# A softmax kernel: tiles of 15, 7 and 3 rows per partition instead of 16, 8 and 4

## The chip, the cores and the metric

The kernel runs on one core of a Trainium2 chip. Its time is the device time of one execution in microseconds. Before the change it is 163.14 us, the median of four runs (163.02 to 163.36). The program is written for the core's engines directly: VectorE (DVE in the profile), ScalarE (ACT), GpSimd (POOL) and SyncE (SP) each run their own list of instructions, TensorE (PE) has no work, and 16 DMA engines move data between HBM and the on-chip memory SBUF, which has 128 partitions.

## The reference

A softmax over the last axis, with a temperature of 2, on 16 x 1024 rows of 512 float32 values:

```python
x_scaled = x / 2.0                      # x: (16, 1024, 512) float32
x_max = np.max(x_scaled, axis=-1, keepdims=True)
exp_x = np.exp(x_scaled - x_max)
return exp_x / np.sum(exp_x, axis=-1, keepdims=True)
```

So 33.55 MB are read once and 33.55 MB written once, and there are 16384 independent rows, 128 for each partition.

## The kernel before, in words

One SBUF tensor, `arena`, holds 100 rows of 512 values per partition (200 KB). Everything happens in place in it: a row is loaded, replaced by its exponentials, scaled, and stored from the same address.

The list `PLAN` (lines 11 to 14) says how the 128 rows of each partition are cut. Each entry is one tile: the rows of its compute chunks, and the row of the arena where it begins. A tile of `r` rows is one load and one store. It takes `r * 128` consecutive rows of the input, and partition `p` gets the `r` consecutive rows `p*r` to `p*r + r - 1` of them (`dram`, a rearrangement "(p r) d -> p r d"). For one partition that is one unbroken piece of HBM, `r` times 2 KB long, and the pieces of neighbouring partitions lie that far apart.

Before the change there are 11 tiles: 4, 8, five times 16, 8, 16, 8 and 4 rows, all computed in chunks of 4 rows. The first eight fill the arena's 100 rows exactly. The last three (16, 8 and 4 rows) use the places of tiles 2, 1 and 0 again: the dictionary `behind` holds, for each tile, the earlier tiles whose place it overlaps.

For each chunk of rows:

- VectorE takes the maximum of each row, negated (`do_max`, line 85: one reduce for the chunk). It waits until the tile's load has landed.
- ScalarE computes exp(0.5 * x + negmax) row by row and gathers each row's sum (line 111). The first row of a chunk waits for the chunk's maximum.
- VectorE takes the reciprocals of the sums (line 94) and multiplies each row by its own (line 98, `do_mul`).

VectorE's order is written out: the maximum of chunk k, then the reciprocals and multiplies of chunk k - 2 (`LAG = 2`).

The transfers are on two queues. The loads of the first eight tiles are issued by ScalarE (line 81), one after the other, before its first exponential. The first two of them are put into the program's entry block ahead of the barrier at which the engines meet. All stores (line 134) are issued by SyncE in tile order, each after a wait for the tile's last multiply. The late loads (line 139) are issued by SyncE too. After the store of tile t, SyncE issues every late load whose overlapped tiles are t - 2 or older, each after a wait for the store of the overlapped tile to have landed. In the kernel before, all three late loads follow the store of tile 4. At the end SyncE waits for all stores.

Everything that a transfer's size, a tile's place and the order of the late loads need is worked out from `PLAN`; no other line knows how long a tile is.

Of the kernel before, what the change touches and what calls it, by code (L numbers as in the profile page):

```python
# [1 line left out]

# [4 lines left out]

PLAN = [
    ([4], 0), ([4, 4], 4), ([4] * 4, 12), ([4] * 4, 28), ([4] * 4, 44), ([4] * 4, 60),
    ([4] * 4, 76), ([4, 4], 92), ([4] * 4, 12), ([4, 4], 4), ([4], 0),
]
ARENA = 100
LAG = 2


@with_exitstack
def kernel(  # L20
    ctx: ExitStack,
    tc: tile.TileContext,
    x: bass.AP,
    out: bass.AP,
):
    nc = tc.nc
    fp32 = mybir.dt.float32

    xf = x.flatten_outer_dims()
    of = out.flatten_outer_dims()  # L30
    N, D = xf.shape
    P = nc.NUM_PARTITIONS
    n_rows = N // P
    assert sum(sum(c) for c, _ in PLAN) == n_rows

    arena = nc.alloc_sbuf_tensor("arena", (P, ARENA, D), fp32)
    negmax = nc.alloc_sbuf_tensor("negmax", (P, n_rows), fp32)
    sums = nc.alloc_sbuf_tensor("sums", (P, n_rows), fp32)
    recip = nc.alloc_sbuf_tensor("recip", (P, n_rows), fp32)

    tiles, chunks, base = [], [], 0
    for t, (cs, at) in enumerate(PLAN):
        r = sum(cs)
        tiles.append((base, r, at))
        o = 0
        for c in cs:
            chunks.append((t, base + o, c, at + o))
            o += c  # L50
        base += r
    last_chunk = {c[0]: k for k, c in enumerate(chunks)}

    def dram(ap, t):
        b, r, _ = tiles[t]
        return ap[b * P : (b + r) * P].rearrange("(p r) d -> p r d", r=r)

    def sb(t):
        _, r, at = tiles[t]
        return arena[:, at : at + r, :]  # L60


    behind = {}
    for t, (_, r, at) in enumerate(tiles):
        for u in range(t):
            _, ru, au = tiles[u]
            if at < au + ru and au < at + r:
                behind.setdefault(t, []).append(u)

    ld = [tc.alloc_semaphore(f"ld{t}") for t in range(len(tiles))]  # L70
    st = [tc.alloc_semaphore(f"st{t}") for t in range(len(tiles))]
    s_max = tc.alloc_semaphore("s_max")
    s_exp = tc.alloc_semaphore("s_exp")
    s_rec = tc.alloc_semaphore("s_rec")
    s_mul = tc.alloc_semaphore("s_mul")

    def issue_loads(begin, end):

        for t in range(begin, end):
            if t not in behind:  # L80
                nc.scalar.dma_start(out=sb(t), in_=dram(xf, t)).then_inc(ld[t], 16)

    def do_max(k):
        t, b, c, a = chunks[k]
        nc.vector.reduce_max(  # L85
            out=negmax[:, b : b + c],
            in_=arena[:, a : a + c],
            axis=mybir.AxisListType.X,
            negate=True,
        )._wait_ge(ld[t], 16).then_inc(s_max, 1)  # L90

    def do_mul(k):
        t, b, c, a = chunks[k]
        nc.vector.reciprocal(  # L94
            out=recip[:, b : b + c], in_=sums[:, b : b + c]
        )._wait_ge(s_exp, k + 1).then_inc(s_rec, 1)
        for r in range(c):
            ins = nc.vector.tensor_scalar_mul(  # L98
                out=arena[:, a + r],
                in0=arena[:, a + r],  # L100
                scalar1=recip[:, b + r : b + r + 1],
            )
            if r == 0:
                ins._wait_ge(s_rec, k + 1)
        ins.then_inc(s_mul, 1)

    def compute_and_store():

        for k, (t, b, c, a) in enumerate(chunks):
            for r in range(c):  # L110
                ins = nc.scalar.activation(  # L111
                    out=arena[:, a + r],
                    in_=arena[:, a + r],
                    func=mybir.ActivationFunctionType.Exp,
                    bias=negmax[:, b + r : b + r + 1],
                    scale=0.5,
                    accum_out=sums[:, b + r : b + r + 1],
                )
                if r == 0:
                    ins._wait_ge(s_max, k + 1)  # L120
            ins.then_inc(s_exp, 1)


        for k in range(len(chunks) + LAG):
            if k < len(chunks):
                do_max(k)
            if k >= LAG:
                do_mul(k - LAG)


        late = sorted(behind)
        for t in range(len(tiles)):
            nc.sync.wait_ge(s_mul, last_chunk[t] + 1)
            nc.sync.dma_start(out=dram(of, t), in_=sb(t)).then_inc(st[t], 16)  # L134
            while late and max(behind[late[0]]) <= t - 2:
                u = late.pop(0)
                for v in behind[u]:
                    nc.sync.wait_ge(st[v], 16)
                nc.sync.dma_start(out=sb(u), in_=dram(xf, u)).then_inc(ld[u], 16)
        for t in range(len(tiles)):  # L140
            nc.sync.wait_ge(st[t], 16)

    hook = nc.inst_callbacks[-1]
    nc.remove_inst_callback(hook)
    symbolic = nc._always_lower_symbolic_ap
    nc._always_lower_symbolic_ap = False
    here = str(nc.cur_bb)
    entry = nc.main_func.blocks[0]  # L150
    head, jumps = entry.instructions[:-5], entry.instructions[-5:]
    entry.instructions = []
    nc.switch_bb("main", None)
    issue_loads(0, 2)
    first = list(entry.instructions)
    at = next(k for k, i in enumerate(head) if type(i).__name__ == "InstDrain")
    entry.instructions = head[:at] + first + head[at:]
    issue_loads(2, len(tiles))
    compute_and_store()
    entry.instructions = list(entry.instructions) + jumps  # L160
    nc.switch_bb(here, None)
    nc._always_lower_symbolic_ap = symbolic
    nc.push_inst_callback(hook)


# [1 line left out]
_INS = ['x']  # L167
_OUTS = [((16, 1024, 512), 'float32')]


# [23 lines left out]
```

## Time and profile before

| | |
|---|---|
| median of 4 runs | 163.14 us (163.02 to 163.36) |
| the profiled execution | 163.47 us, of which the span is 161.7 us |
| VectorE busy | 127.0 us (79%), 192 instructions |
| ScalarE busy | 95.0 us (59%), 257 instructions |
| DMA | 67.14 MB, mean 415 GB/s over the span |
| reduce of a chunk of 4 rows (line 85) | 32 of 2279 ns |
| multiply of a row (line 98) | 128 of 481 ns |
| exponential of a row (line 111) | 128 of 710 ns, and 187 ns to read its sum |

The profile shows one execution. "Busy" counts the time in which an engine runs an instruction. In lines that describe a group of instructions, the part after the last bar is the engine's idle time just before them and what ended it. A queue's share is the time of its packets as a part of 16 DMA engines' span; a packet is what one DMA engine moves in one go. In the lines of transfers the last number is the time from issue to landing, which includes the time in which the transfer stands behind others in its queue. In a table of stretches the columns are: begin and end, length, busy time (and count) of VectorE, ScalarE and GpSimd, TensorE's granted clock, the DMA engines' share, and GB/s.

### The profile page before, as it was taken

To read this page: it belongs to the slowest core of one execution; us is meant where nothing else is said; L and a number is where in the kernel's file an instruction comes from. 1 tells how busy PE (TensorE), PEld (TensorE's weight loads), DVE (VectorE), ACT (ScalarE), POOL (GpSimd) and SP (SyncE) were. 2 spreads that over 40 slices of the span, in tenths; PEclk is the share of its full clock that TensorE was granted. 3 is DMA by queue.
4 is the path that set the end of the run, shared out by engine and by line. 5 is a ranking of instruction groups with operands and counts; after the bars stand their busy time and mean duration, and the time that the engine had idled before them with its cause. 6 is when DMAs were issued, how large, how long until landed. Compare 5 with 4: busy or idle time off the path is not lost.

```text
span 161.7 us, 518 instructions
## 1 busy us (share of the span) xinstructions
DVE 127.0 (79%) x192; ACT 95.0 (59%) x257; POOL 0.2 (0%) x4
## 2 busy tenths in 40 slices
DVE  0559199999999999999966999998999999920000
ACT  0559457777777777777771777775777777600000
POOL 0000000000000000000000000000000000000000
DMA  6999999999989999999999999999999999999993
GB/s 243 462 462 389 401 466 454 367 397 462 462 375 503 389 422 446 438 413 422 462 405 409 458 422 440 413 442 389 373 434 454 430 422 420 446 434 446 397 407 136
DMA packets 3172, 67.14 MB, mean 415 GB/s; under 512 B 352, under 2 KB 352, under 8 KB 352
## 3 DMA queue, kind: packets, MB, share of 16 engines
q1 hardware_dynamic: 2016, 40.90, 59.3%
q10 hardware_dynamic: 1152, 26.21, 38.3%
q14 instruction: 4, 0.03, 0.0%
HBM read 33.55 MB, written 33.55 MB: 415 GB/s over the span
## 4 chain that ended last, share of the span: by engine, by line
DVE 54%; DMA 33%; issue 0%; DVEq 0%; SPq 0%
DMA arena<-in_x_dram 33%; DVE negmax L85 29%; DVE arena L98 24%; DVE recip L94 1%; DVEq L189 0%; SPq L134 0%
## 5 line engine op out<-in xcount | busy, mean ns | idle before, releaser
L111 ACT ACTIVATE arena<-arena,negmax 128x512 f32<-128x512 f32 x128 | 90.8, 710 | 40.8 <-DVE negmax L85 40.8
L85 DVE TENSOR_REDUCE negmax<-arena 128x4 f32<-128x2048 f32 x32 | 72.9, 2279 | 14.4 <-DMA arena<-in_x_dram 14.4
L98 DVE TENSOR_SCALAR arena<-arena,recip 128x512 f32<-128x512 f32 x128 | 53.6, 481 | 1.1
L111 ACT ACTIVATION_READ_ACCUMULATOR arena<-arena,negmax 128x1 f32 x128 | 23.9, 187 | 0.0
L94 DVE RECIPROCAL recip<-sums 128x4 f32<-128x4 f32 x32 | 5.4, 168 | 0.0
L111 ACT ACT_TABLE_LOAD x1 | 1.3, 1283 | 4.3 <-issue 4.3
L178 POOL MEMSET const-bfloat16-1.0<- 128x1 bf16 x1 | 0.1, 103 | 0.0
L178 POOL MEMSET const-uint8-127<- 128x1 uint8 x1 | 0.1, 102 | 0.0
L178 POOL MEMSET const-float32-0.0<- 128x1 f32 x1 | 0.1, 98 | 0.2 <-issue 0.2
L178 POOL MEMSET const-float32-1.0<- 128x1 f32 x1 | 0.1, 98 | 0.0
## 6 DMA issues: line engine op xcount, KB each, us to landing
out_dram<-arena SPq DMA_DIRECT2D x6, 4096.0 KB, 26.3
arena<-in_x_dram ACTq DMA_DIRECT2D x5, 4096.0 KB, 45.1
out_dram<-arena SPq DMA_DIRECT2D x3, 2048.0 KB, 20.4
arena<-in_x_dram ACTq DMA_DIRECT2D x2, 2048.0 KB, 53.3
arena<-in_x_dram SPq DMA_DIRECT2D x1, 4096.0 KB, 35.0
out_dram<-arena SPq DMA_DIRECT2D x2, 1024.0 KB, 17.6
arena<-in_x_dram SPq DMA_DIRECT2D x1, 2048.0 KB, 38.5
arena<-in_x_dram ACTq DMA_DIRECT2D x1, 1024.0 KB, 4.8
```

Of the source, the lines that this page charges most:

```text
L85: nc.vector.reduce_max(out=negmax[:, b : b + c], in_=arena[:, a : a + c], axis=mybir.AxisListType.X, negate=True,)._wait_ge(ld[t], 16).the ...
L94: nc.vector.reciprocal(out=recip[:, b : b + c], in_=sums[:, b : b + c])._wait_ge(s_exp, k + 1).then_inc(s_rec, 1)
L98: ins = nc.vector.tensor_scalar_mul(out=arena[:, a + r], in0=arena[:, a + r], scalar1=recip[:, b + r : b + r + 1],)
L111: ins = nc.scalar.activation(out=arena[:, a + r], in_=arena[:, a + r], func=mybir.ActivationFunctionType.Exp, bias=negmax[:, b + r : b + r ...
L178: nc = _bacc.Bacc("TRN2", target_bir_lowering=False, num_devices=1)
```

## The change

Only `PLAN` changes. The tiles become 3, 7, six times 15, 15, 7, 3 and 3 rows: twelve instead of eleven. The chunks have 5 rows in the 15-row tiles, 4 and 3 in the 7-row tiles, and 3 in the 3-row tiles: 28 chunks instead of 32. The first eight tiles again fill the arena's 100 rows and are loaded by ScalarE. The four late tiles (15, 7, 3 and 3 rows) use the places of tiles 2, 1 and 0 and the first three rows of tile 3's place. By the rule for late loads, the first three follow the store of tile 4, and the twelfth tile's load follows the store of tile 5.

```diff
 PLAN = [
-    ([4], 0), ([4, 4], 4), ([4] * 4, 12), ([4] * 4, 28), ([4] * 4, 44), ([4] * 4, 60),
-    ([4] * 4, 76), ([4, 4], 92), ([4] * 4, 12), ([4, 4], 4), ([4], 0),
+    ([3], 0), ([4, 3], 3), ([5] * 3, 10), ([5] * 3, 25), ([5] * 3, 40), ([5] * 3, 55),
+    ([5] * 3, 70), ([5] * 3, 85), ([5] * 3, 10), ([4, 3], 3), ([3], 0), ([3], 25),
 ]
```

## The prediction

> **What bounds the kernel now.** I read four views in this order: the slices, to see which resource never rests; the queues and transfers, to see what it carries; the stretches, to find where it loses time; then the chain of waits and the store issues, to see whether compute ever starves it.
>
> The slices (40 of 4.04 us each; digits are tenths of busy time):
>
> ```profile
> DVE  0559199999999999999966999998999999920000
> ACT  0559457777777777777771777775777777600000
> DMA  6999999999989999999999999999999999999993
> DMA packets 3172, 67.14 MB, mean 415 GB/s; under 512 B 352, under 2 KB 352, under 8 KB 352
> ```
>
> The DMA row is full from the second slice to the last but one, while VectorE falls silent four slices before the end. The 16 DMA engines are the bound; VectorE's end is not the kernel's. The chain that ended last gives "DVE 54%", but it ends in the last multiply at 142.5 us, with 19 us of span to come, so I don't take it for the bound.
>
> The queues and transfers (q10 is ScalarE's queue: the first eight loads; q1 is SyncE's: all stores and the late loads):
>
> ```profile
> q1 hardware_dynamic: 2016, 40.90, 59.3%
> q10 hardware_dynamic: 1152, 26.21, 38.3%
> ...
> out_dram<-arena SPq DMA_DIRECT2D x6, 4096.0 KB, 26.3
> arena<-in_x_dram ACTq DMA_DIRECT2D x5, 4096.0 KB, 45.1
> ```
>
> 59.3% + 38.3% = 97.6% of 161.7 us: 157.8 us of packets on each engine. The trace's packet records show one packet per partition and transfer (8, 16 or 32 KB, eight per engine), with medians of 309, 611 and 1213 ns, and 9 ns for each semaphore packet. The three lie on a line: (1213 - 309)/3 = 301.3 ns for 8 KB, and 309 - 301.3 = 7.7 ns fixed.
>
> The ideal sum for one engine is then 32 x 309 + 48 x 611 + 96 x 1213 + 22 x 9 = 155.86 us. The rest of the span: the first packet starts at 1.15; packets above their median add 2.12 us per engine; engines without a packet, about 0.3. That makes 159.4, where the last store's sixteen landings have their mean (159.43); the slowest engine lands at 160.60; 1.08 us of closing waits follow: 161.7. So the change can act through the packet sum, the 2.4 us of slow packets and gaps, or the 1.17 us by which the slowest engine trails the mean, unless it starves the DMA.
>
> The stretches (us; the last two columns are DMA share and GB/s):
>
> ```profile
> 63.00:96.00 33.00, 30.09 (x45) 22.21 (x62) 0.00 (x0) 1.00 1.01 433
> ...
> 113.00:115.00 2.00, 1.97 (x7) 1.74 (x5) 0.00 (x0) 1.00 0.93 397
> 115.00:117.00 2.00, 2.00 (x2) 1.19 (x4) 0.00 (x0) 1.00 1.04 344
> 117.00:119.00 2.00, 1.97 (x7) 1.75 (x5) 0.00 (x0) 1.00 1.10 463
> 119.00:135.00 16.00, 15.86 (x26) 11.77 (x33) 0.00 (x0) 1.00 1.00 432
> ```
>
> Steady traffic makes 432 or 433 GB/s. The largest dip is at 115 to 117, 344 GB/s at a full share. That is the last late load (tile 10, 4 rows), alone on q1 between another load and the store of tile 5: 30 of its 128 packets take 319 to 1048 ns instead of 309. Mean landings of the two loads lie 3.19 us apart (114.96 and 118.15) where 8 packets need 2.48: 0.7 us lost. The spread of the sixteen landings grows there from 1.48 to 2.32 us, and every store after it keeps 2.3.
>
> Last, waits and two store issues:
>
> ```profile
> DVE negmax L85 <- DMA arena<-in_x_dram: 14.4, 5, 5.0
> ...
> 110.18 0.34 SPq L134 DMA_DIRECT2D out_dram<-arena  x1
> ...
> 134.99 0.33 SPq L134 DMA_DIRECT2D out_dram<-arena  x1
> ```
>
> Tile 6's store is issued at 110.18, while its predecessor in the ring lands at 129.1; tile 8's at 134.99, its predecessor at 143.6. The least slack late in the run is thus 8.6 us.
>
> **The change, part by part.**
>
> *Packets.* The bytes stay. Now 3-, 7- and 15-row tiles give packets of 6, 14 and 30 KB: by the line above 234, 535 and 1138 ns, an estimate from those three medians. Per engine: 6 transfers of 3 rows (48 x 233.7 = 11.22), 4 of 7 (32 x 535.0 = 17.12), 14 of 15 (112 x 1137.7 = 127.42), 24 semaphore packets (0.22): 155.97 us, +0.11. All of it is on the path.
>
> A rule speaks louder against more and smaller transfers: the Trainium skill, "DMA: Bandwidth & Descriptors", section "Rules for kernel authors", wants at least 1 MiB per DMA, and its "Anatomy of one DMA" gives each a fixed 2 us or so. The 3-row transfers are 0.75 MiB, and two transfers are added: by that rule an estimated +4 us, 167. The row says otherwise: transfers queue behind one another and the DMA share stays at 1.00 across their borders, so the fixed time is covered, and I take 0.11. It would show only if a ring ran dry.
>
> *A twelfth tile.* Its 3 rows go to row 25 of the arena, so its load waits for the store of tile 3. SyncE issues that load after store 5 and ahead of store 6; on q1 it lies between two stores. The nearest row is the dip above: a small load on q1 alone, with a store behind it, lost 0.7 us on the mean engine. Bounds: nothing, if that dip was tied to its moment; 1.1 us, what the slowest engine lost there (last landings 3.57 us apart against 2.48). I take the row, scaled to 3 rows of 4: +0.5. Gains are not excluded for the traffic as a whole, but for these 3 rows I see no reason for one.
>
> The wait itself: behind it on SyncE stand store 6 and later ones. Store 5 needs 70 rows computed. By the chain, 4 rows take 2.19 + 0.10 + 0.03 + 1.68 = 4.0 us of VectorE, so 70 rows are ready near 90. Store 3 covers 40 rows, where the present one covers 44 and landed at 86.3. The semaphore is up; price nothing, and store 6 has over 10 us in hand were it late.
>
> *Starvation.* VectorE does one row per 1.0 us, the DMA one per 1.21 (load plus store). With 5-row chunks, a reduce lies between 2279 ns (the 4-row price) and 2849 (in proportion); four chunks fewer save small fixed costs, hidden under DMA. The waits move: tile 7 has 15 rows, not 8. Loads arrive at one row per 1.2 us while stores share evenly, so tile 6 lands near 80 and tile 7 near 98; VectorE comes to them near 76 and 95 and waits about 4 us each, against 2.7 and nothing now. Store 6 is then issued near 109, store 7 near 124, store 8 near 137, the last near 146. On q1, when q10 ends near 98, the ring holds 25 late rows, store 5 (15) and the twelfth load (3): 43 x 0.607 us = 26, to 124. Store 6 then lasts to 133, store 7 to 142. So store 8 has about 5 us in hand rather than 8.6. Price nothing; with 6 us more of waiting, each further us would be a us of time.
>
> *Start and end.* The first load is 3 rows: VectorE starts some 0.6 us earlier, which nothing waits for, because q10 keeps the engines full. The first packet still starts at 1.15. One more final wait costs about 0.03.
>
> *Addresses.* Partitions now lie 30 KB apart in HBM, not 32. The row: slow packets come in clusters where a transfer starts or ends (18.9, 29.4 to 33.5, 97 to 100 us), 1.1 us per engine outside the first burst and the dip at 115. If they come from streams stepping together at power-of-two distances, they could go, with part of the 1.17 us of spread: a gain of 0 to 2.3. [...] The trace has 433 GB/s at 32 KB, and most packets at their median. [...] The other way, a packet that isn't a multiple of 8 KB might be slower; no row has one; 1% on the 30 KB packets would cost 1.3 us. Between these I take 0, where the rows of full rate stand.
>
> Sum: +0.11 + 0.5 + 0.03 = +0.64 on the profiled span, 161.7 to 162.3. The profiled execution took 163.47, so 1.8 us lie around the span; it was 0.33 above the median of the runs. Added to that median: 163.14 + 0.64 = 163.8 us.
>
> **The rivals.**
>
> *The odd pitch pays.* For it: the clusters, in which all 16 engines are slow at once, and the lag of the slowest engine. Against it: tile 2's load also starts in step on all engines, without slow packets. Half of clusters and lag gives -1.15, with the +0.64 above: 162.6; all of it, with a harmless twelfth load: 161.0. It decides once 0.97 us is won (0.64 + 0.33).
>
> *The twelfth load is free* and the dip was a matter of its moment: +0.14, 163.3; within 0.2% (0.33 us, about what a measurement of this kernel can tell from no change).
>
> *The DMA starves or the odd packets are slow.* VectorE's longer waits push store 8 past 142, or 30 KB packets lose 1%: 165 or more. Against it: 5 us of slack and the straight line of packet times.
>
> **How the numbers follow.** Slower by the sum (163.5 to 164.4): 0.44; free twelfth load: 0.18; pitch pays: 0.31; starvation or slow packets: 0.07. The likeliest gives 163.8, with its own range 163.5 to 164.4. The range for 8 in 10 takes in most of the pitch case: 162.0 to 164.6. Faster 0.31; same 0.18; slower 0.51.
>
> **What would show it.** Right: packets, less the slow ones, at 234, 535 and 1138 ns; a DMA row full to the end; a second dip in GB/s near 122 to 126, where the twelfth load runs; last landings spread by over 2.3 us. Wrong: no slow packets near transfer borders and a spread under 1.5 us (the pitch), or a slice of the DMA row below 9 between 100 and 150 us (starvation). The forecast fails if packet times leave their line, since each 1% of them weighs 1.6 us.

## The result and the profile after

The changed kernel takes 162.78 us (median of 44 runs, 162.14 to 164.08) against 163.40 of the kernel before in the same sessions (63 runs): a ratio of 0.9966, 95% interval 0.9954 to 0.9977. It is 0.34% faster, where 163.8 us, 0.64 us more than before, was forecast. The median lies inside the range of 162.0 to 164.6, but on the other side of "no change". Its profiled execution has a span of 160.8 us, against 161.7. A few executions take 2 us or more longer, whatever the kernel (166.53 and 166.84 us among the 63), and the ratios leave these out.

The slices of the changed kernel, with its packet count:

```profile
DVE  0475599999999999999799919999999999950000
ACT  0739087866697666886287634668766875600000
DMA  7999999999999999999999999999999999999993
DMA packets 3459, 67.13 MB, mean 418 GB/s; under 512 B 384, under 2 KB 384, under 8 KB 1152
```

The DMA row is full again, now without the one slice of 8 that the kernel before has. VectorE shows a deep hole in its 24th slice and still ends before the DMA. So the bound is the same, and nothing starved it.

The queues and transfers of the changed kernel:

```profile
q1 hardware_dynamic: 2304, 40.90, 59.3%
q10 hardware_dynamic: 1152, 26.21, 38.7%
...
out_dram<-arena SPq DMA_DIRECT2D x7, 3840.0 KB, 26.1
arena<-in_x_dram ACTq DMA_DIRECT2D x6, 3840.0 KB, 48.1
```

By the packet records of these two queues, an engine has 157.53 us of packets, where it had 157.93. The sum by the measured medians (234, 535 and 1138 ns) rises by 0.16 us, so it is the slow packets that became fewer or shorter: 1.50 us per engine lie above the medians instead of 2.06.

The stretches of the changed kernel (DMA share and GB/s at the end). Its late load of tile 10 lands at 113.47 us, so the place to compare is 111 to 113, not 115 to 117:

```profile
63.00:96.00 33.00, 27.97 (x43) 21.82 (x60) 0.00 (x0) 1.00 1.01 433
...
109.00:111.00 2.00, 2.00 (x6) 2.00 (x7) 0.00 (x0) 1.00 0.92 388
111.00:113.00 2.00, 2.00 (x1) 1.07 (x4) 0.00 (x0) 1.00 1.20 492
113.00:115.00 2.00, 1.97 (x6) 1.63 (x5) 0.00 (x0) 1.00 1.00 430
...
119.00:121.00 2.00, 2.00 (x5) 2.00 (x7) 0.00 (x0) 1.00 0.78 335
121.00:123.00 2.00, 2.00 (x1) 0.93 (x4) 0.00 (x0) 1.00 1.19 501
123.00:125.00 2.00, 1.96 (x7) 1.77 (x5) 0.00 (x0) 1.00 0.98 418
125.00:127.00 2.00, 2.00 (x2) 1.86 (x6) 0.00 (x0) 1.00 1.00 430
```

A packet is counted where it starts, so neighbours must be read together: 388 and 492 make 440 GB/s. In the kernel before, 397, 344 and 463 from 113 to 119 make 401. The landings say it more sharply: tiles 9 and 10 land on the mean 1.95 us apart, where their packets need 1.88; before it was 3.19 against 2.48. The dip is gone. Nor is there one where the twelfth load runs: 335 and 501 make 418 GB/s, and 418 and 430 follow.

VectorE's waits for loads and two store issues of the changed kernel:

```profile
DVE negmax L85 <- DMA arena<-in_x_dram: 15.7, 5, 4.6
...
105.70 0.34 SPq L134 DMA_DIRECT2D out_dram<-arena  x1
...
133.68 0.33 SPq L134 DMA_DIRECT2D out_dram<-arena  x1
```

Store 8 is issued at 133.68; its predecessor in the ring (the queue's list of packets) lands at 142.70. That is 9 us in hand, no less than before.

The account that the rest of this document uses splits each profile's end into four parts. A transfer lands on each of the 16 engines at its own time; the mean is over the sixteen. "Lag at tile 9" is the mean landing of that late load, less the first packet's start and less its own packets and all those queued ahead of it, by their medians. "Dip" is what the next load, tile 10, adds to that lag. "Rest" is what is added until the last store's mean landing. "Last" is how far the slowest DMA engine trails that mean.

| profile | lag at tile 9 | dip | rest | last | span |
|---|---|---|---|---|---|
| before | 1.84 | 0.71 | -0.13 | 1.17 | 161.7 |
| before, again (e1) | 2.22 | 0.65 | -0.13 | 1.12 | 162.0 |
| after | 1.64 | 0.07 | -0.26 | 1.08 | 160.8 |
| after, again (e2) | 1.60 | 0.08 | -0.28 | 0.89 | 160.6 |
| after, third (e16) | 1.64 | 0.09 | -0.25 | 1.66 | 161.4 |

By their means: lag -0.41, dip -0.60, rest -0.13, last +0.07, first packet and packets +0.16. The sum is -0.91 us; the mean spans differ by -0.90. So the gain has two main parts: 0.60 us is one event of some 2 us length, 0.41 is spread over the 110 us before it. These few profiles show more than the times do, whose medians differ by 0.62 us. Two profiles of the kernel before differ by 0.38 in their lag alone, so the part of the dip is the surer one.

### The profile page after: what moved, and what is told of

It reads as the page before. It is cut to its first block, busy times and chain, and to the rows that moved or that the text cites. A ratio compares the mean times of both kernels' runs of the same rounds, so it can differ in the third digit from the quotient of the medians.

```text
span 160.8 us, 513 instructions
## 1 busy us (share of the span) xinstructions
DVE 126.3 (79%) x184; ACT 94.5 (59%) x257; POOL 0.2 (0%) x4
## 4 chain that ended last, share of the span: by engine, by line
DVE 74%; DMA 10%; another core or an unknown queue 3%; issue 0%; DVEq 0%
DVE negmax L85 40%; DVE arena L98 32%; DMA arena<-in_x_dram 10%; DVE recip L94 2%; DVEq L189 0%
## 5 line engine op out<-in xcount | busy, mean ns | idle before, releaser
L85 DVE TENSOR_REDUCE negmax<-arena 128x5 f32<-128x2560 f32 (+2 forms) x28 | 72.3, 2585 | 15.7 <-DMA arena<-in_x_dram 15.7
L94 DVE RECIPROCAL recip<-sums 128x5 f32<-128x5 f32 (+2 forms) x28 | 4.9, 176 | 0.0
```

The source lines that it names most:

```text
L85: nc.vector.reduce_max(out=negmax[:, b : b + c], in_=arena[:, a : a + c], axis=mybir.AxisListType.X, negate=True,)._wait_ge(ld[t], 16).the ...
L94: nc.vector.reciprocal(out=recip[:, b : b + c], in_=sums[:, b : b + c])._wait_ge(s_exp, k + 1).then_inc(s_rec, 1)
```

## The experiments

All kernels here are read in the same account. Times are ratios to the kernel before, run on the same chip in the same session.

### Does the dip come every time?

e1 is the kernel before and e2 the changed kernel, both unchanged. e1 and, further down, e9 are single executions; the others were timed 4 to 13 times.

> The kernel before, unchanged, for a second profile. Three theories of the 0.9 us of span that the change won. LATE LOAD: the gain is the vanished dip at the late 4-row load (tile 10), where the kernel before fell 0.7 us behind its packet sum. PITCH: the 15-row tiles cure slow packets along the whole run. MOMENT: the dip was an accident of one execution. LATE LOAD expects the dip here again: mean landings of tiles 9 and 10 about 3.2 us apart (2.48 by the packets), some 30 slow 8 KB packets, spread of the last landings 2.3 us. PITCH expects slow packets again before 100 us (1.1 us per engine), the dip either way. MOMENT expects 2.5 us between the two landings and a last spread near 1.5.

Measured: span 162.0 us, dip 0.65 us, last landings spread over 2.36 us. The stretches of this second profile:

```profile
113.00:115.00 2.00, 1.97 (x6) 1.33 (x4) 0.00 (x0) 1.00 0.94 401
115.00:117.00 2.00, 2.00 (x3) 1.60 (x6) 0.00 (x0) 1.00 0.98 340
117.00:119.00 2.00, 1.97 (x6) 1.35 (x4) 0.00 (x0) 1.00 1.09 434
```

340 GB/s at the same place, where the first profile had 344: the theory of a mere moment falls.

> The changed kernel, unchanged, for a second profile and a time on the same chip as the two kernels beside it. All theories: ratio to before 0.9966 or so (0.995 to 0.998). LATE LOAD and PITCH: no dip at tiles 10 and 11 again (mean landings of tiles 9 and 10 within 0.1 us of the 1.88 that the packets need). MOMENT: a dip may appear at any place.

Measured: 162.83 us, ratio 0.9963 (0.9942 to 0.9983), dip 0.08 us, span 160.6.

### Is it the late load's size?

e3 gives the kernel before a late load of 3 rows; e4 gives the changed kernel one of 4 rows.

```diff
 # e3, on the kernel before
-    ([4] * 4, 76), ([4, 4], 92), ([4] * 4, 12), ([4, 4], 4), ([4], 0),
+    ([4] * 4, 76), ([4, 4], 92), ([4] * 4, 12), ([5, 4], 3), ([3], 0),
 # e4, on the changed kernel
-    ([5] * 3, 70), ([5] * 3, 85), ([5] * 3, 10), ([4, 3], 3), ([3], 0), ([3], 25),
+    ([5] * 3, 70), ([5] * 3, 85), ([5] * 3, 10), ([3, 3], 4), ([4], 0), ([3], 25),
```

> The kernel before with one thing changed: the late tiles have 16, 9 and 3 rows instead of 16, 8 and 4, so the last late load is the 3-row load of the changed kernel; everything before it keeps 16, 8 and 4. LATE LOAD: most of the gain comes back, ratio 0.996 (0.994 to 0.998), the landings of tiles 9 and 10 are 1.9 us apart, last spread under 1.9. PITCH: no gain, ratio 1.000 (0.998 to 1.002), slow packets before 100 us as before. MOMENT: ratio 1.000.

> The changed kernel with one thing changed: the late tiles have 15, 6, 4 and 3 rows instead of 15, 7, 3 and 3, so the last load ahead of store 5 is a 4-row one with 8 KB packets, as in the kernel before; the twelfth tile stays. LATE LOAD: the gain is lost, ratio near 1.000 (0.998 to 1.002), the landings of tiles 9 and 10 are 3.1 us apart instead of 2.48. PITCH: the gain stays, ratio 0.9966, landings 2.5 us apart. MOMENT: as the changed kernel, 0.9966.

Measured: e3 has a ratio of 0.9997 (0.9970 to 1.0024), a dip of 0.67 us and a lag of 2.15; e4 has 0.9958 (0.9938 to 0.9979), a dip of 0.06 and a lag of 1.62. Both go against the theory of the late load. The size of that load, 3 or 4 rows, does nothing to the mean; the gain stays with the 15-row tiles. The same stretches of e3, with 6 KB packets in the dip:

```profile
113.00:115.00 2.00, 1.97 (x6) 1.52 (x5) 0.00 (x0) 1.00 0.95 409
115.00:117.00 2.00, 2.00 (x2) 1.41 (x4) 0.00 (x0) 1.00 1.02 322
117.00:119.00 2.00, 1.97 (x6) 1.53 (x5) 0.00 (x0) 1.00 1.18 465
```

### Is it the packets or the addresses?

e5 and e6 keep all sizes and the order, and change only which rows of HBM a tile takes: each partition owns 128 consecutive rows, so the pieces of all tiles lie 256 KB apart. e7 does the like on e3, with 250 KB for all tiles but the last, tile 10, whose pieces keep to 6 KB.

```diff
 # e5 on the kernel before, e6 on the changed kernel
-        return ap[b * P : (b + r) * P].rearrange("(p r) d -> p r d", r=r)
+        return ap.rearrange("(p n) d -> p n d", p=P)[:, b : b + r, :]
 # e7 on e3
+        if b + r <= 125:
+            return ap[: 125 * P].rearrange("(p n) d -> p n d", p=P)[:, b : b + r, :]
         return ap[b * P : (b + r) * P].rearrange("(p r) d -> p r d", r=r)
```

> The kernel before with another cut of the HBM side alone: every partition owns 128 consecutive rows, so all tiles have a pitch of 256 KB between partitions; packets, tile sizes, order and waits stay. Three theories of what the 15-row tiles cure, now that the size of the late load is out. PITCH: streams that step together at a power-of-two distance collide; 256 KB is a higher power of two, so it is as slow as before or slower: ratio 1.000 to 1.02, dip at 115 to 117 us as before or deeper. PACKET: it is the 32 KB packets (or the 30 KB ones) whatever the address; ratio 1.000 (0.998 to 1.002). STORE BEHIND: the dip comes from the 16-row store that follows the late load; ratio 1.000, dip as before.

> The changed kernel with the same other cut: a pitch of 256 KB for all tiles, 15-row tiles and 30 KB packets as they are. PITCH: the gain is lost, ratio equal to that of the kernel before with 256 KB (1.000 to 1.02), a dip and clusters of slow packets like those of the kernel before. PACKET and STORE BEHIND: the gain stays, ratio 0.996 (0.994 to 0.998), no dip.

> The kernel before with late tiles of 16, 9 and 3 rows (0.9997 of before), and the HBM side cut so that each partition owns 125 consecutive rows for all tiles but the last: a pitch of 250 KB, no power of two, with 32 KB packets and all else kept. PITCH: the gain appears without any 15-row tile: ratio 0.996 (0.994 to 0.998), no dip at 115 to 117 us. PACKET and STORE BEHIND: ratio 1.000 (0.997 to 1.002), the dip stays.

| | ratio | lag at tile 9 | dip |
|---|---|---|---|
| e5: 16 rows, 256 KB | 0.9969 (0.9945 to 0.9992) | 1.66 | 0.37 |
| e6: 15 rows, 256 KB | 0.9992 (0.9971 to 1.0013) | 1.66 | 0.29 |
| e7: 16 rows, 250 KB | 0.9993 (0.9971 to 1.0015) | 1.78 | 0.52 |

The changed kernel gets a dip back as soon as its addresses change, with the very same packets; on the slowest engine it is 1.26 us (last landings of tiles 9 and 10 at 111.56 and 114.70, less 1.88). The stretches of e6 show it at 111 to 113:

```profile
109.00:111.00 2.00, 2.00 (x4) 2.00 (x7) 0.00 (x0) 1.00 0.95 385
111.00:113.00 2.00, 1.99 (x2) 0.71 (x3) 0.00 (x0) 1.00 1.08 393
113.00:115.00 2.00, 1.97 (x5) 2.00 (x6) 0.00 (x0) 1.00 1.05 455
```

So the dip depends on where the rows lie in HBM, and packet size alone does not decide. At 256 KB the two kernels have the same lag and nearly the same dip, and the 15-row tiles are even slower (163.38 us in e6 against 162.97 in e5, same session): 15 rows win nothing there by themselves. But it isn't "powers of two" either: stores 250 KB apart keep the dip, and the kernel before became faster at 256 KB, where that theory said slower or equal. No theory had expected that. The lag at tile 9 is 1.84 to 2.22 us in the profiles with 16-row pieces 32 KB apart, and 1.66 and 1.78 with the other two pitches, on one profile each: by these, the smaller part of the gain comes with getting away from pieces 32 KB apart, not with 15 rows.

How far apart the engines are before the load does not decide either: the sixteen landings of tile 9 spread over 1.48 us in the kernel before, 1.43 in e6, and 1.90 in e11 below, which has no dip.

### What makes the dip?

e8 gives tile 5, whose store stands right behind the last late load, 15 rows in the kernel before (and tile 7 nine). e9 makes SyncE hold that store back until the load has landed.

```diff
 # e8
-    ([4] * 4, 60), ([4] * 4, 76), ([4, 4], 92),
+    ([5] * 3, 60), ([4] * 4, 75), ([5, 4], 91),
 # e9
             nc.sync.wait_ge(s_mul, last_chunk[t] + 1)
+            if t == 5:
+                nc.sync.wait_ge(ld[10], 16)
```

> The kernel before with two sizes changed: tile 5 has 15 rows instead of 16, tile 7 has 9 instead of 8; the store of tile 5, which stands behind the last late load, then has 30 KB pieces at a 30 KB pitch. STORE BEHIND: the dip at 115 to 117 us goes (mean landings of tiles 9 and 10 2.5 us apart), ratio 0.997 (0.995 to 0.999). PACKET: only one tile in six differs, ratio 0.9995, dip stays. PITCH: the dip goes if the store is its half of the collision, and stays if the load alone makes it.

> The kernel before, where SyncE holds the store of tile 5 back until the last late load (tile 10) has landed, so that no write to HBM is under way while that load is read. SWITCH (the dip is made by engines that already write tile 5 while others still read tile 10): the slow 8 KB packets at 115 to 117 us go, tiles 9 and 10 land 2.5 us apart on the mean, and the span grows only by the DMA's rest between the two, some 2 us, to 163 to 165. LOAD ALONE (small packets slow by themselves): some 30 slow packets stay.

e9 is the clearest run of the study. Its dip is -0.02 us, and the packets of 8 KB on q1 exceed their median by 0.04 us per engine instead of 0.50. The wait and the stretches of e9:

```profile
SPq L135 <- DMA arena<-in_x_dram: 38.9, 1, 38.9
...
115.00:117.00 2.00, 2.00 (x3) 1.90 (x6) 0.00 (x0) 1.00 0.90 381
117.00:119.00 2.00, 1.97 (x5) 1.04 (x3) 0.00 (x0) 1.00 0.24 98
```

SyncE stands 38.9 us in front of store 5 and issues it at 119.05, where the kernel before does so at 94.23. The engines run dry from 117 on (share 0.24), which costs more than the dip: span 163.8. But the load's packets keep their pace to the end. So, by this one execution, the load alone is not slow; it is slow when the store stands behind it in the ring. How the store does it is not shown. The theory named engines that already write while others still read. But in the kernel before, the lengthened packets start between 115.25 and 117.8 us, and the first packet of store 5 at 116.72: a third of the loss (0.16 of 0.49 us per engine) lies in packets that had ended by then, and only 0.05 in packets that started later.

e8's time was 0.9980 (0.9948 to 1.0012); repeated as e15 it was 0.9974 (0.9957 to 0.9991). The executions profiled were longer than that (span 164 and 166 us), and show a dip of about 0.5 us; what a shorter one has is not known.

> The kernel before with 15 rows in tile 5 and 9 in tile 7 once more, since its first profile was of a disturbed execution. TILE PITCH: dip under 0.1 us between tiles 9 and 10, ratio 0.997. BASE PARITY: dip of 0.4 to 0.6 us (all regions up to tile 5 still begin on multiples of 1 MB), ratio 0.998 to 1.000.

By the time, one tile of 15 rows in place of 16 wins about 0.2%, between the theories; by these two profiles it doesn't cure the dip. It settles nothing.

### Loads or stores?

e10 and e11 give the 256 KB pitch to one side only, in the changed kernel. Their output has its rows in another order; the work is the same.

```diff
+        if ap is xf:    # e10; e11: "if ap is of"
+            return ap.rearrange("(p n) d -> p n d", p=P)[:, b : b + r, :]
         return ap[b * P : (b + r) * P].rearrange("(p r) d -> p r d", r=r)
```

> The changed kernel with loads cut at a pitch of 256 KB between partitions and stores as they are (30, 14 and 6 KB): the rows of the output come out in another order, the work is the same. LOAD SIDE (the addresses that are read make the dip): a dip at tile 10 as with 256 KB on both sides (0.3 us on the mean, last landing 1.2 us late), ratio 0.999. STORE SIDE: no dip (under 0.1 us), ratio 0.9965. BOTH (only the pair of patterns counts): neither is full.

> The changed kernel with stores cut at a pitch of 256 KB and loads as they are; the rows of the output come out in another order, the work is the same. LOAD SIDE: no dip, ratio 0.9965. STORE SIDE: the dip of 256 KB on both sides, ratio 0.999.

Measured: e10 0.9965 (0.9936 to 0.9994), dip 0.01 us; e11 1.0006 (0.9976 to 1.0036), dip 0.05. Neither side alone brings the dip back. Both sides together do (e6). So, on one profile each, it is a matter of reads and writes against each other. One pair of runs doesn't fit a rule of the pitches alone: e7 and e11 both load tile 10 in 6 KB pieces and store 250 or 256 KB apart, yet e7 with 16 rows has a dip of 0.52 us and e11 with 15 rows 0.05. That e11 has no dip and yet no gain I can't explain by the dip: its slowest engine trails the mean by 1.55 us, against 0.9 to 1.7 in the changed kernel, and its interval still reaches into that of the changed kernel.

### The place of the regions

e12 takes the rows of tile 10 from the front of HBM in the kernel before. e13 shifts the beginnings of the regions of tiles 2 to 7 and 10 to odd multiples of 256 KB (tile 8, which the expectation counts in, stays on a multiple of 1 MB), by a 7-row tile 1, a 9-row tile 7 and late tiles of 16, 7, 4 and 1. e14 orders the changed kernel's regions so that those of tiles 5 and 10 begin at multiples of 1 MB.

```diff
 # e12
+        b = 0 if t == len(tiles) - 1 else b + tiles[-1][1]
 # e13
+    ([4], 0), ([4, 3], 4), ([4] * 4, 11), ([4] * 4, 27), ([4] * 4, 43), ([4] * 4, 59),
+    ([4] * 4, 75), ([5, 4], 91), ([4] * 4, 11), ([4, 3], 4), ([4], 0), ([1], 27),
 # e14
+        order = [2, 3, 4, 6, 5, 7, 8, 1, 10, 0, 9, 11]
+        b = sum(tiles[u][1] for u in order[: order.index(t)])
```

> The kernel before with the HBM rows of tile 10 taken from the front of the input and output (all other tiles move up by 4 rows per partition, 1 MB); pitch, packets, order and waits stay. BASE (the dip needs the exact 16 MB between the region that tile 10 reads and the one that tile 5 writes): dip gone, ratio 0.997. PATTERN (pitch of the pieces, wherever the region lies): dip as before, 0.6 us, ratio 1.000.

> The kernel before with 16-row tiles and 32 KB pitch kept, but tile 1 one row shorter, tile 7 one longer and the late tiles 16, 7, 4 and 1: the regions of all 16-row tiles and of tile 10 begin at odd multiples of 256 KB in HBM instead of multiples of 1 MB. BASE PARITY (a region that begins on a multiple of 1 MB makes the dip): dip under 0.1 us, ratio 0.997. TILE PITCH (the store of tile 5 with pieces 32 KB apart makes it): dip of 0.4 to 0.7 us, ratio 1.000.

> The changed kernel with its tiles' regions in another order in HBM, so that the region of tile 5 (stored behind the late load) begins at 60 rows per partition and that of tile 10 (the late load) at 112, both multiples of 1 MB as in the kernel before; pitch, packets, order and waits stay. BASE PARITY: a dip of 0.3 us or more at tile 10, ratio 0.999. TILE PITCH: no dip, 0.9965.

| | ratio | lag at tile 9 | dip | last |
|---|---|---|---|---|
| e12 | 1.0002 (0.9969 to 1.0035) | 1.94 | 0.41 | 0.95 |
| e13 | 1.0118 (1.0097 to 1.0139) | 1.93 | 0.54 | 3.07 |
| e14 | 0.9943 (0.9925 to 0.9962) | 1.51 | 0.02 | 1.39 |

Moving the load's region (e12) does not remove the dip, odd beginnings (e13) don't either, and even ones (e14) don't bring it. Where these two regions begin does not decide it, though e12 and e13 have a somewhat smaller dip. e13 loses 1.2% in another way: its mean engine ends at 159.41 us, as that of the kernel before, but its slowest lands at 162.48. Its slices, whose last two tell:

```profile
DMA  7999989998999999999999999999999999999970
GB/s 236 430 455 481 389 371 459 426 441 383 476 443 401 481 409 393 489 393 409 481 400 410 419 497 385 409 422 412 420 453 416 417 449 387 471 419 417 422 327 28
```

In the kernel before, the row ended in "407 136" GB/s; here it ends in "327 28". Fourteen engines are done at 159.38 us, and two carry on, to 161.89 and 162.48.

Since e14 looked faster than the changed kernel, both were run side by side.

> The changed kernel, unchanged, as the measure for the kernel beside it on the same chip: ratio 0.9965 (0.995 to 0.998). Third profile: no dip at tile 10, lag of tile 9's landing behind its packets 1.6 us.

> The changed kernel with its tiles' regions in another order in HBM, once more, to see if it beats the changed kernel. ORDER HELPS: ratio to before 0.9945 (0.993 to 0.996), 0.2% under the kernel beside it, slow packets at the starts of loads fewer than there (1.2 us per engine in all against 1.6). NO EFFECT: ratio 0.9965, equal to the kernel beside it, and the first result was the scatter of five runs.

Measured: e16 163.05 us, 0.9971 (0.9952 to 0.9990); e17 162.75 us, 0.9949 (0.9921 to 0.9978), lag 1.60, dip 0.04, slow packets 1.31 us per engine against 1.62 in e16. The medians lie 0.18% apart, but the intervals overlap widely: an advantage of that order of regions isn't shown.

## Why the prediction was wrong

*What bounds the kernel.* Right. The DMA's row stayed full, and VectorE's longer waits cost nothing.

*Packets.* Right to the nanosecond: medians 234, 535 and 1138 ns. By these whole nanoseconds the sum is 0.16 us higher, where 0.11 was forecast. The estimate of +4 us, weighed against the row and put aside, came from a fixed cost of about 2 us a transfer. The Trainium skill ("DMA: Bandwidth & Descriptors", "Anatomy of one DMA — SWDGE (gpsimd) path") gives that for transfers that GpSimd issues; here ScalarE and SyncE issue all of them, and two more transfers cost nothing visible.

*A twelfth tile, +0.5.* This step failed. Its load lands 1.82 us behind store 5 on the mean (121.61 and 123.43), where its packets need 1.88: it cost nothing. The row was the right place to look at, but I read its loss as a property of a small load with a store behind it. e3 and e4 show that the size is indifferent, and the changed kernel has the same order of load and store at tiles 10 and 11 without the loss. By e5, e6, e10 and e11 the loss depends on where the rows read and written lie in HBM, which this change alters. I had carried a cost of the old layout over to a new one, and at tile 10 the same cost, 0.6 us, was about to vanish.

*Addresses, 0 out of a range of 0 to 2.3.* This step failed too: by e5 and e6 the gain came from here, about -1.0 us (lag -0.41, dip -0.60). I took 0 because most packets stand at their median. That was the wrong row for the question: the lengthened packets decide, and they added 2.1 us. The range was made of the clusters outside the dip (1.1 us) and the spread (1.17). Of the clusters at most the 0.41 of the lag was won, and of the spread nothing: the slowest engine trails by 1.2 us before and after, on the mean of the profiles. What wasn't seen is that the dip, left out of the range and priced under another step as if it were fixed, is one more such cluster, and the largest after the first burst. With these three sizes in place (0 for +0.5, and -0.41 and -0.60 for 0) the prediction's own sum is -0.87 us on the span, and the profiles differ by -0.90.

*The rival "the odd pitch pays"* gave 162.6 for half of the clusters and lag with the twelfth load at its price; 162.78 was measured. That is near by luck: its twelfth load cost 0.5 us that was not there, and its gain left out the dip. Its reason, power-of-two distances, fell: 256 KB on both sides made the kernel before faster, not slower, and stores 250 KB apart left the dip. The Trainium skill's row on large powers of two (same page, "Latency and other measured facts", "HBM row pitch at large powers of two") begins at 512 KiB, still with 207 GB/s where full rate is 214, and falls to half at 4 MiB; no run here went there, and at 256 KB nothing of the kind is seen.

*Starvation.* Right in sign, too careful in size. Tiles 6 and 7 landed at 77.5 and 95.7 us, not near 80 and 98. VectorE's waits for them were 1.47 and 3.35 us rather than 4 each, and store 8 had 9 us in hand, not 5.

*What would show it.* The forecast of a second dip at 122 to 126 and of a spread over 2.3 us failed (the spread was 1.69, 1.50 and 2.27 in three profiles). The sign named for the pitch, a spread under 1.5 us and no slow packets near borders, didn't come in full either: slow packets remain at the borders, only fewer of them.

*What stays open.* Which relation of read and write addresses makes the dip, and how a store slows the load ahead of it before its own first packet starts. By these runs it isn't the load's size, the beginning of the two regions, or a power of two as such, and in the changed kernel neither side's pitch alone. That the store tile's size has a part is neither shown nor excluded (e7 and e11 speak for it, e5 and e6 against it).

## What to carry to other kernels

When a kernel keeps its DMA engines full, add up the packets by their medians and look at what is left over. The slow packets, with time and place, and the engine that ends last are what a change of tiling can still win, and a large part may be one event. A loss that a trace shows at one place is not a price per event. Before it is carried over to a new event, ask which properties of the old place the change keeps; here it did not keep the HBM layout.

## What the runs showed that I had not expected

The last load of a batch is slowed by a store that stands behind it in the ring: by 0.4 to 0.7 us on the mean engine and 0.6 to 1.4 on the slowest, in all seven profiles of the kernel with 16-row tiles in which the store was not held back (before, e1, e3, e5, e7, e12 and e13). In the six of the changed kernel whose pieces are as far apart as its tiles are long (after, e2, e4, e14, e16 and e17) it is at most 0.1 on the mean, and 0.1 to 0.8 on the slowest.

The same packets in the same order move by about 0.3% with the HBM layout alone: 1 and 0.9969 (0.9945 to 0.9992) for the 16-row tiles. For the 15-row tiles it is 0.9966 and 0.9992, whose intervals just touch (0.9954 to 0.9977 and 0.9971 to 1.0013).

One or two engines' lateness can cost as much as all slow packets: in e13 the mean engine was as fast as before, and the slowest one lost 1.9 us more, which is the whole 1.2%. Why these two engines trail is not known.
